# Sums of the way down's blocks: added to the residual on VectorE straight from PSUM

## The chip, the cores and the metric

The kernel runs on one core of a Trainium2 chip. The metric is device time in microseconds (us), the median of three runs. In the profile PE is TensorE's matrix multiplication and PEld its weight loads, DVE is VectorE, ACT ScalarE, POOL GpSimd, SP SyncE (which here only issues transfers). One execution was taken by the hardware profiler; its rows are used below.

## The reference, cut to what matters

One layer of a streaming encoder runs over 1152 tokens (1024 of a new stream and 8 x 16 of running ones): a half step of a gated feed-forward network, a mixer (gated delta rule beside a pooling branch), a second half step, and a final normalization.

```python
x = x + 0.5 * swiglu(rms_norm(x, norm_ffn1), w_ffn1_gate, w_ffn1_up, w_ffn1_down)
x = x + mixer(rms_norm(x, norm_mix), ...)
x = x + 0.5 * swiglu(rms_norm(x, norm_ffn2), w_ffn2_gate, w_ffn2_up, w_ffn2_down)
y = rms_norm(x, norm_final)

def swiglu(x, w_gate, w_up, w_down):
    return (silu(x @ w_gate) * (x @ w_up)) @ w_down
```

The model is 1024 wide and the hidden layer 2816. The change lies in the product with `w_down`, called the way down here, of both half steps, and in the last line, the final normalization.

## The kernel before, in words

Tokens are cut into three chunks: chunk 0 with 512 columns, chunks 1 and 2 with 320 each. Everything is kept transposed, features on the 128 partitions and tokens along the free axis, so the residual is a tile `xk(c, d)` of 128 x 512 or 128 x 320 for each chunk c and feature block d (0 to 7). Every float32 product is made from three products of a reduced type: a weight and an activation are each split into a high part and a remainder (`piece`: an ACT cast at L287 and a DVE subtraction at L288 for weights).

A way down has two halves. `down0` does chunk 0 in the plain way, its sums in the PSUM tag `d`. `down12` does chunks 1 and 2 together by a scheme that makes a 2 x 2 block product from seven products instead of eight (`DOWN` names their seven right sides). It has 12 units: three groups of hidden blocks (`GROUPS`, of 4, 3 and 4) times four feature blocks d. In a unit each of the seven products is 12 matmuls (9 in the middle group) of 128 x 320. Three PSUM tags take them: `a` (`al`, into which four of the products are added one after another, `B11`, `T2`, `T3`, `T4`), `b` (`ga`, product `B21`) and `c` (`be`, products `T1` and then `B22`). After each product the partial sum so far is added to one residual tile: chunk 1 or 2, block d or d + 4, with factor 0.5 or -0.5. Because `al` and `be` go on accumulating, the next product into the same tile starts only after the sum so far has been read.

These seven additions a unit are made in two ways. Five are one DVE instruction that reads PSUM and the residual tile and writes the residual tile (`add`, L652 and L653). Two go another way: after `T1`, ACT copies -0.5 x `be` to a buffer `c3` (L648) and POOL adds it (L649); after `B11`, ACT copies 0.5 x `al` to a buffer `p1` (L677) and POOL adds that (L678). Both buffers lie in region R2 and in Q or A5.

POOL also makes the sums of weight blocks that the scheme needs: three at L282 (the blocks of `T1`, `T3` and `B22`) and one at L286 (for `T2`), four a unit. They need the unit's two weight transfers (`load`), whose buffers come free when the last piece of the unit two before has been split. The product `T1` of the next unit (`fifth`) and `T4` of the one before (`left_low`) are written between the products of the current unit, so each unit's order on PE is T1 of the next unit, T3, B11, B21, T4 of the one before, T2, B22.

`final(c)` does the last line of the reference for chunk c once its squares are summed: `rstd_rest` makes the reciprocal root (two small groups of matmuls with a POOL power between them, L232) and ACT copies it to an SBUF row `r` (L237); then each of the eight tiles is scaled by weight and root, three of them on ACT and POOL (L1568, L1569) and five in one DVE instruction (L1571), and written to `y_out` (L1572). For chunk 0 this is stepped from `beside` inside the second `down12`; for chunks 1 and 2 it is the end of the program.

The order of the instructions on each engine is set by the tile framework's scheduler from the order in which the program names them; each engine then runs its own list strictly in order. `tc.issue_after(ins)` puts the instructions of its block behind `ins` on that instruction's engine.

Of the kernel before, what the change touches and what calls it, by code (L numbers as in the profile page):

```python
# [7 lines left out]
F32 = mybir.dt.float32  # L8
F32R = mybir.dt.float32r
AF = mybir.ActivationFunctionType  # L10
ALU = mybir.AluOpType
# [5 lines left out]
KT = D // P  # L17
# [23 lines left out]
def trunk(ctx: ExitStack, tc: tile.TileContext, xin, s0, convst, poolst, cm_in, vec_in, small_in,  # L41
# [3 lines left out]
    V, A, G, T, SY = nc.vector, nc.scalar, nc.gpsimd, nc.tensor, nc.sync  # L45
# [30 lines left out]
    def pt(tag, shape=None):  # L76
        t = psum.tile([P, 512], F32, tag=tag, name=nm("ps_" + tag))
        return t
# [16 lines left out]
    def region(tag, dt=F32):  # L95
        return main.tile([P, SIZE[tag]], dt, tag=tag, name=nm(tag))
# [17 lines left out]
    def xk(c, k):  # L114
        return X[c][k // 4][:, k % 4, :]
# [149 lines left out]
    N = CHUNKS[1][1]  # L265
    N0 = CHUNKS[0][1]

    class Blocks:
# [5 lines left out]
        def piece(self, *src, more=None):  # L274

            m = src[0].shape[-1]
            t = region(self.ring[self.n % len(self.ring)], F32R)
            self.n += 1
            hi, lo = t[:, :m], t[:, 512:512 + m]
            if len(src) == 2:  # L280
                t = self.gs.get("s", m)
                G.tensor_add(t, *src)  # L282
                src = [t]
            src = src[0]
            if more:
                G.tensor_add(more[0], src, more[1])  # L286
            A.copy(hi, src)  # L287
            V.tensor_sub(lo, src, hi.bitcast(F32))  # L288
            return [x.rearrange("p (k c) -> p k c", c=P) for x in (hi, lo)]

        def product(self, ps, w, hs, start=True, stop=True):
# [316 lines left out]
    def down12(wd, gk, op0, beside, done):  # L608
# [3 lines left out]
        gs, piece, product = bl.gs, bl.piece, bl.product  # L612
        for tag in ("R0", "R1", "O5", "O6"):
            gs.place(region(tag), ("raw", 1024, 1))
        gs.place(region("R2"), ("p1", N, 2), ("c3", N, 1))

        def temps(tag):
            for t in ("s", "sum"):
                gs.mem.pop(t, None)
            gs.mem["c3"] = gs.mem["c3"][:1]  # L620
            gs.place(region(tag), ("s", 512, 2), ("sum", 512, 1), ("c3", N, 1))

        ops = {0: op0}

# [18 lines left out]

        def fifth(g, d, w):

            be, sm, c3 = pt("c")[:, :N], gs.get("sum", w[0].shape[-1]), gs.get("c3", N)
            product(be, piece(w[2], w[3], more=(sm, w[0])), ops[g]["T1"], True, False)
            A.mul(c3, be, -0.5)  # L648
            G.tensor_add(xk(2, d + 4), xk(2, d + 4), c3)  # L649
            return be, sm  # L650

        def add(c, d, ps, by=0.5):  # L652
# [16 lines left out]
        for u, (g, d) in enumerate(units):  # L669
            if not nxt:  # L670
                w = load(g, d, 6)
                nxt = w, fifth(g, d, w)
            (a11, a12, a21, a22), (be, sm) = nxt
            op = ops[g]
            al, ga, p1 = pt("a")[:, :N], pt("b")[:, :N], gs.get("p1", N)
            product(al, piece(a11), op["B11"])
            A.mul(p1, al, 0.5)  # L677
            G.tensor_add(xk(1, d), xk(1, d), p1)  # L678
            product(ga, piece(a12), op["B21"])
            next(beside, None)  # L680
            if last:
# [11 lines left out]
            if u + 1 < len(units):  # L693
# [3 lines left out]
                w = load(g2, d2, 6 if g2 == 0 else 10)  # L697
# [7 lines left out]
            last = g, d, al, a22  # L705
# [749 lines left out]
    for n in names:  # L1455
        if n[1] in "dHXr":
            continue
        b, w, h = n[0], n[1], n[2]
# [79 lines left out]
    squares = {}  # L1538
# [19 lines left out]
    def final(c):  # L1558
        o, n = CHUNKS[c]
        last = c > 0  # L1560
        pool = (2, 5) if last else (1, 4, 7)
        r = nt[c].get("nsq", n)
        pr = yield from rstd_rest(n, squares[c], r)
        yield
        for k in range(KT):
            x, w = xk(c, k), vec[:, 24 + k:25 + k]
            if k in pool:
                A.mul(x, x, w)  # L1568
                G.tensor_tensor(x, x, r, ALU.mult)  # L1569
            else:  # L1570
                V.scalar_tensor_tensor(x, x, w, pr if last else r, ALU.mult, ALU.mult)  # L1571
            (A if last and k in pool else SY).dma_start(y_out[:, o * KT + k * n:o * KT + (k + 1) * n], x)  # L1572
            yield

    downs(wd2, g_keep, x_keep, lambda d: square(0, d), final, square)
# [92 lines left out]
```

## Time and profile before

| | us |
|---|---|
| median of three runs (2211.72 to 2213.26) | 2213.12 |
| the profiled execution | 2211.95 |
| its span, first to last instruction | 2210.2 |
| `down12` of the first half step | about 648 to 790 in the span |
| `down12` of the second half step | about 2040 to 2194 in the span |

The span is what the rows below divide; the profiled execution's own time is 1.75 us longer. A row of the timeline gives the start in the span, the length, the engine, the line of the kernel, the tiles written and read, the count of instructions put together, and in brackets how long the engine sat idle before it and who ended that.

### The profile page before, as it was taken

What the parts mean: (1) busy time and instruction counts of PE and PEld (TensorE: products, weight loads), DVE (VectorE), ACT (ScalarE), POOL (GpSimd) and SP (SyncE); (2) the same over time, 40 slices, a digit from 0 to 9 for tenths busy, and PEclk for the clock granted to TensorE, in tenths of its full rate; (3) what the DMA queues carried; (4) which work ended last, traced back from release to release, by engine and by line L of the source; (5) the groups of instructions that cost most, each with busy time, mean ns of one, the idle gap of its engine ahead of it and who ended that gap; (6) DMA issues with size and microseconds to landing.
All of it is one profiled execution on the core that took longest, in us unless ns stands there. A gap on an engine that the chain in (4) does not pass through costs nothing.

```text
span 2210.2 us, 33211 instructions
## 1 busy us (share of the span) xinstructions
PE 2134.5 (97%) x12341; PEld 1922.0 (87%) x12341; DVE 1519.3 (69%) x2685; ACT 937.0 (42%) x1905; POOL 734.0 (33%) x667
## 2 busy tenths in 40 slices
PE   8999999999999899999999998999999999999997
PEld 7899999998889877787889887889999999988897
DVE  7866666677345867778687867786666668744775
ACT  6433333444223554545444443543333334423343
POOL 1433333440025522322232333143333344101663
PEclk9999999999999999999999999999999999999998
DMA  6332333554555522121222122442333346446561
GB/s 250 114 126 102 130 109 116 182 198 149 189 181 202 190 77 68 49 66 52 77 80 80 44 92 93 135 142 96 124 106 130 109 145 237 141 148 214 183 250 67
DMA packets 102386, 289.72 MB, mean 131 GB/s; under 512 B 16208, under 2 KB 24272, under 8 KB 101968
## 3 DMA queue, kind: packets, MB, share of 16 engines
q1 hardware_dynamic: 101648, 286.94, 38.6%
q8 instruction: 97, 1.59, 0.3%
q10 hardware_dynamic: 576, 0.66, 0.1%
q14 instruction: 65, 0.53, 0.1%
HBM read 214.89 MB, written 72.66 MB: 130 GB/s over the span
## 4 chain that ended last, share of the span: by engine, by line
PE 78%; DVE 10%; issue 3%; POOL 3%; DMA 3%; ACT 2%; DVEq 0%; SPq 0%; POOLq 0%; ACTq 0%
PE ps_a L58 28%; PE ps_b L58 19%; PE ps_d L58 17%; PE ps_c L58 13%; DVE O L288 2%; DMA R<-in_wd 1%; DVE B L982 1%; DVE O L186 1%; DVE A L1122 1%; DVE x L653 1%; PE ps_b L62 1%; DVE A L1324 1%; POOL Q L282 1%; POOL A L282 1%; POOL x L678 1%
## 5 line engine op out<-in xcount | busy, mean ns | idle before, releaser
L58 PE MATMUL ps_a<-B,O 128*128 128x320 f32 x3040 | 510.6, 312 | 16.3 <-DVE x L653 13.2
L58 PEld LDWEIGHTS ps_a<-B,O 128*128 128x128 f32 x3040 | 466.8, 189 | 29.0 <-ACT O L287 15.6
L58 PE MATMUL ps_a<-A,O 128*128 128x320 f32 (+1 forms) x1952 | 426.4, 354 | 3.1 <-DVE A L1122 1.6
L58 PEld LDWEIGHTS ps_a<-A,O 128*128 128x128 f32 x1952 | 330.2, 190 | 37.8 <-issue 3.9
L288 DVE TENSOR_TENSOR O<-Q,O 128x512 fp32r<-128x512 f32 (+1 forms) x238 | 216.5, 913 | 193.6 <-ACT O L287 189.6
L58 PE MATMUL ps_b<-A,O 128*128 128x512 f32 (+1 forms) x1128 | 263.8, 388 | 7.4 <-ACT O L287 7.4
L58 PEld LDWEIGHTS ps_b<-A,O 128*128 128x128 f32 x1128 | 209.0, 189 | 47.1 <-ACT O L287 7.4
L58 PE MATMUL ps_d<-A,O 128*128 128x512 f32 x1056 | 244.1, 391 | 2.3 <-DVE x L602 1.4
L58 PEld LDWEIGHTS ps_d<-A,O 128*128 128x128 f32 x1056 | 196.9, 188 | 48.4 <-issue 3.6
L287 ACT CAST O<-Q 128x512 fp32r<-128x512 f32 (+1 forms) x238 | 143.2, 604 | 187.6 <-POOL Q L282 47.5
L288 DVE TENSOR_TENSOR O<-R,O 128x512 fp32r<-128x512 f32 (+1 forms) x216 | 200.3, 931 | 32.5 <-ACT O L287 31.8
L58 PE MATMUL ps_d<-B,O 128*128 128x320 f32 (+1 forms) x1104 | 205.2, 331 | 5.4 <-DVE x L1003 3.7
L282 POOL TENSOR_TENSOR Q<-R 128x512 f32<-128x512 f32 (+1 forms) x44 | 58.4, 1328 | 433.2 <-DVE O L288 149.0
L287 ACT CAST O<-R 128x512 fp32r<-128x512 f32 (+1 forms) x216 | 130.9, 611 | 134.5 <-PE ps_a L58 54.5
L58 PE MATMUL ps_c<-A,O 128*128 128x512 f32 (+1 forms) x816 | 186.9, 377 | 1.1 <-DVE O L288 1.1
L58 PEld LDWEIGHTS ps_d<-B,O 128*128 128x128 f32 x1104 | 171.2, 189 | 16.0 <-DVE x L1003 6.1
L58 PEld LDWEIGHTS ps_c<-A,O 128*128 128x128 f32 x816 | 145.6, 188 | 25.0 <-DVE O L288 1.9
L185 ACT CAST O<-R 128x1024 fp32r<-128x1024 f32 (+1 forms) x86 | 85.9, 1010 | 183.0 <-PE ps_d L58 136.5
L58 PE MATMUL ps_c<-B,O 128*128 128x320 f32 x912 | 145.8, 310 | 3.0 <-DVE O L288 1.9
L58 PEld LDWEIGHTS ps_c<-B,O 128*128 128x128 f32 x912 | 136.9, 188 | 4.1 <-DVE O L288 2.4
L393 POOL TENSOR_TENSOR A<-A,A 128x512 fp32r<-128x512 f32 x44 | 72.4, 1646 | 161.1 <-ACT A L392 161.0
L186 DVE TENSOR_TENSOR O<-R,O 128x1024 fp32r<-128x1024 f32 (+1 forms) x74 | 87.4, 1188 | 50.3 <-ACT O L185 29.7
(318 smaller groups left out, 3116.4 us busy)
## 6 DMA issues: line engine op xcount, KB each, us to landing
g_keep<-x SPq DMA_DIRECT2D x98, 320.0 KB, 2.5
R<-in_wg SPq DMA_DIRECT2D x48, 512.0 KB, 3.8
R<-in_wd SPq DMA_DIRECT2D x48, 512.0 KB, 3.7
R<-in_wu SPq DMA_DIRECT2D x47, 512.0 KB, 3.7
g_keep<-A SPq DMA_DIRECT2D x44, 512.0 KB, 2.6
A<-g_keep SPq DMA_DIRECT2D x44, 512.0 KB, 5.5
B<-g_keep SPq DMA_DIRECT2D x56, 320.0 KB, 6.6
A<-g_keep SPq DMA_DIRECT2D x42, 320.0 KB, 5.0
```

The lines of the kernel that those rows point to most:

```text
L58: self.put(nc.tensor.matmul(out, lhs, rhs, **k), n / 2400 + .003 if lhs.dtype == F32R else max(n, lhs.shape[-1]) / 600)
L62: self.put(nc.tensor.transpose(out, lhs, rhs), out.shape[-1] / 1200)
L185: A.copy(hi, raw)
L186: (e or V).tensor_sub(lo, raw, hi.bitcast(F32))
L282: G.tensor_add(t, *src)
L287: A.copy(hi, src)
L288: V.tensor_sub(lo, src, hi.bitcast(F32))
L393: G.tensor_sub(go[:, 1], sg, go[:, 0].bitcast(F32))
L653: V.scalar_tensor_tensor(xk(c, d), ps, by, xk(c, d), ALU.mult, ALU.add)
L678: G.tensor_add(xk(1, d), xk(1, d), p1)
L982: V.scalar_tensor_tensor(y[:, :512], raw[:, t:t + 512], cw[:, t:t + 1], y[:, :512], ALU.mult, ALU.add)
L1122: V.tensor_tensor(Uc[:, :, m + 1:], Uc[:, :, m + 1:], tu[:, :n, :w], ALU.add)
```

## The change

Three things change. In `down12` the additions after `T1` and `B11` become `add` like the other five, so all seven are DVE instructions that read PSUM; the two ACT copies and the two POOL additions of a unit go, and with them the buffers `c3` and `p1` (a second buffer `sum` takes the place of one). In `final`, chunk 0 no longer uses ACT and POOL: its eight tiles are all scaled on DVE, each put behind the `piece` subtraction that was named last (`Blocks.mark`), and the step is spread over two more turns of `beside`. At the end of the program three transfers of chunk 1 are issued by ACT instead of SP.

```diff
@@ piece
-            V.tensor_sub(lo, src, hi.bitcast(F32))
+            Blocks.mark = V.tensor_sub(lo, src, hi.bitcast(F32)).ins
@@ down12
-        gs.place(region("R2"), ("p1", N, 2), ("c3", N, 1))
 
         def temps(tag):
             for t in ("s", "sum"):
                 gs.mem.pop(t, None)
-            gs.mem["c3"] = gs.mem["c3"][:1]
-            gs.place(region(tag), ("s", 512, 2), ("sum", 512, 1), ("c3", N, 1))
+            gs.place(region(tag), ("s", 512, 2), ("sum", 512, 2))
@@ down12.fifth
-            be, sm, c3 = pt("c")[:, :N], gs.get("sum", w[0].shape[-1]), gs.get("c3", N)
+            be, sm = pt("c")[:, :N], gs.get("sum", w[0].shape[-1])
             product(be, piece(w[2], w[3], more=(sm, w[0])), ops[g]["T1"], True, False)
-            A.mul(c3, be, -0.5)
-            G.tensor_add(xk(2, d + 4), xk(2, d + 4), c3)
+            add(2, d + 4, be, -0.5)
@@ down12, a unit
-            al, ga, p1 = pt("a")[:, :N], pt("b")[:, :N], gs.get("p1", N)
+            al, ga = pt("a")[:, :N], pt("b")[:, :N]
             product(al, piece(a11), op["B11"])
-            A.mul(p1, al, 0.5)
-            G.tensor_add(xk(1, d), xk(1, d), p1)
+            add(1, d, al)
             product(ga, piece(a12), op["B21"])
@@ final
-        pool = (2, 5) if last else (1, 4, 7)
+        pool = (2, 5) if last else ()
         r = nt[c].get("nsq", n)
-        pr = yield from rstd_rest(n, squares[c], r)
+        root = rstd_rest(n, squares[c], r)
+        next(root)
+        if not last:
+            yield
+            yield
+        yield
+        pr = yield from root
         yield
         for k in range(KT):
             x, w = xk(c, k), vec[:, 24 + k:25 + k]
             if k in pool:
                 A.mul(x, x, w)
                 G.tensor_tensor(x, x, r, ALU.mult)
+            elif last:
+                V.scalar_tensor_tensor(x, x, w, pr, ALU.mult, ALU.mult)
             else:
-                V.scalar_tensor_tensor(x, x, w, pr if last else r, ALU.mult, ALU.mult)
-            (A if last and k in pool else SY).dma_start(y_out[...], x)
+                with tc.issue_after(Blocks.mark):
+                    V.scalar_tensor_tensor(x, x, w, r, ALU.mult, ALU.mult)
+            (A if last and (k in pool or c == 1 and k % 2) else SY).dma_start(y_out[...], x)
             yield
```

The first place is POOL's list at the first units of the first `down12`. Q holds the sums of weight blocks, R and O the raw weights, x the residual; L649 and L678 are the two additions. Before:

```order
L649 TENSOR_TENSOR x_488_5204<-x_488_5204,R_522_5463 128x320
L282 TENSOR_TENSOR Q_5464<-O_521_5462 128x512
L282 TENSOR_TENSOR Q_5464<-R_518_5459,R_519_5460 128x512
L286 TENSOR_TENSOR Q_5464<-Q_5464,O_520_5461 128x512
L678 TENSOR_TENSOR x_485_5201<-x_485_5201,R_522_5463 128x320
L282 TENSOR_TENSOR Q_5464<-Q_5464,O_520_5461 128x512
L649 TENSOR_TENSOR x_488_5204<-x_488_5204,Q_5464 128x320
L282 TENSOR_TENSOR Q_5464<-R_519_5460 128x512
L282 TENSOR_TENSOR Q_5464<-O_520_5461,O_521_5462 128x512
```

Now:

```order
L282 TENSOR_TENSOR Q_5463<-O_521_5462 128x512
L286 TENSOR_TENSOR Q_5463<-Q_5463,O_520_5461 128x512
L282 TENSOR_TENSOR Q_5463<-R_518_5459,R_519_5460 128x512
L282 TENSOR_TENSOR Q_5463<-Q_5463,O_520_5461 128x512
L282 TENSOR_TENSOR Q_5463<-R_519_5460 128x512
L282 TENSOR_TENSOR Q_5463<-O_520_5461,O_521_5462 128x512
L286 TENSOR_TENSOR Q_5463<-Q_5463,R_518_5459 128x512
```

Between the sums of weight blocks nothing is left; two L282 have changed places with an L286.

The second place is DVE's list in the second unit there. L288 is the subtraction of a piece (O is the ring of split weights), L653 an addition from PSUM, which is L650 in the changed kernel. Before, from the piece of the next unit's T1 on:

```order
L288 TENSOR_TENSOR O_550_5706<-Q_5464,O_550_5706 128x512
L653 SCALAR_TENSOR_TENSOR x_485_5201<-ps_b_5614,x_485_5201 128x320
L288 TENSOR_TENSOR O_551_5725<-Q_5464,O_551_5725 128x512
L653 SCALAR_TENSOR_TENSOR x_486_5202<-ps_a_5500,x_486_5202 128x320
L288 TENSOR_TENSOR O_554_5744<-R_518_5459,O_554_5744 128x512
L653 SCALAR_TENSOR_TENSOR x_487_5203<-ps_a_5613,x_487_5203 128x320
L288 TENSOR_TENSOR O_555_5761<-R_518_5459,O_555_5761 128x512
L653 SCALAR_TENSOR_TENSOR x_487_5203<-ps_c_5576,x_487_5203 128x320
L288 TENSOR_TENSOR O_556_5776<-O_521_5462,O_556_5776 128x512
```

Now, from the addition after B11 on:

```order
L650 SCALAR_TENSOR_TENSOR x_485_5201<-ps_a_5609,x_485_5201 128x320
L288 TENSOR_TENSOR O_549_5701<-Q_5463,O_549_5701 128x512
L650 SCALAR_TENSOR_TENSOR x_485_5201<-ps_b_5610,x_485_5201 128x320
L288 TENSOR_TENSOR O_550_5719<-Q_5463,O_550_5719 128x512
L650 SCALAR_TENSOR_TENSOR x_486_5202<-ps_a_5498,x_486_5202 128x320
L288 TENSOR_TENSOR O_553_5738<-R_518_5459,O_553_5738 128x512
L650 SCALAR_TENSOR_TENSOR x_487_5203<-ps_a_5609,x_487_5203 128x320
L288 TENSOR_TENSOR O_554_5754<-R_518_5459,O_554_5754 128x512
L650 SCALAR_TENSOR_TENSOR x_487_5203<-ps_c_5573,x_487_5203 128x320
L288 TENSOR_TENSOR O_555_5769<-O_521_5462,O_555_5769 128x512
```

The addition after B11 (`ps_a_5609`) stands ahead of the piece of the next T1, and the addition after B21 (`ps_b_5610`) behind that piece, as it stood before; the addition after the next T1 (`ps_c`) follows the last piece shown.

The third place is DVE's list in the second `down12`, where chunk 0's tiles are scaled (L1571 before, L1576 now; R is the row of roots). Before:

```order
L653 SCALAR_TENSOR_TENSOR x_1831_17673<-ps_c_17966,x_1831_17673 128x320
L288 TENSOR_TENSOR O_1894_18152<-R_1864_17946,O_1894_18152 128x512
L1571 SCALAR_TENSOR_TENSOR x_1381_12581<-x_1381_12581,vec,R_1841_17742 128x512 x3
L1571 SCALAR_TENSOR_TENSOR x_1382_12582<-x_1382_12582,vec,R_1841_17742 128x512
L288 TENSOR_TENSOR O_1895_18168<-Q_17950,O_1895_18168 128x512
L653 SCALAR_TENSOR_TENSOR x_1832_17674<-ps_a_17986,x_1832_17674 128x320
L288 TENSOR_TENSOR O_1896_18185<-Q_17950,O_1896_18185 128x512
L1571 SCALAR_TENSOR_TENSOR x_1382_12582<-x_1382_12582,vec,R_1841_17742 128x512
L288 TENSOR_TENSOR O_1898_18213<-Q_17950,O_1898_18213 128x512
```

Now:

```order
L288 TENSOR_TENSOR O_1897_18196<-Q_17924,O_1897_18196 128x512
L1576 SCALAR_TENSOR_TENSOR x_1380_12556<-x_1380_12556,vec,R_1840_17717 128x512 x2
L650 SCALAR_TENSOR_TENSOR x_1829_17647<-ps_a_17959,x_1829_17647 128x320
L288 TENSOR_TENSOR O_1900_18217<-R_1862_17920,O_1900_18217 128x512
L650 SCALAR_TENSOR_TENSOR x_1830_17648<-ps_a_18078,x_1830_17648 128x320
L288 TENSOR_TENSOR O_1901_18233<-R_1862_17920,O_1901_18233 128x512
L1576 SCALAR_TENSOR_TENSOR x_1380_12556<-x_1380_12556,vec,R_1840_17717 128x512
L650 SCALAR_TENSOR_TENSOR x_1830_17648<-ps_c_18042,x_1830_17648 128x320
L288 TENSOR_TENSOR O_1902_18250<-O_1865_17923,O_1902_18250 128x512
```

Before, four of the scalings stand together and a fifth three rows later; now there are two and then one, and the other five follow singly, each behind a later piece of the next two units.

## Rows read from the trace of the kernel before

**Rows 1.** Busy us, share and instructions by engine, from the page

```profile
PE 2134.5 (97%) x12341; PEld 1922.0 (87%) x12341; DVE 1519.3 (69%) x2685; ACT 937.0 (42%) x1905; POOL 734.0 (33%) x667
```

**Rows 2.** Stretches: busy us of PE, PEld, DVE, ACT, POOL; clock, DMA, GB/s

```profile
648.00:790.00 142.00, 128.67 (x835) 123.96 (x834) 100.02 (x151) 63.28 (x123) 82.81 (x69) 0.99 0.53 182
...
2040.00:2194.00 154.00, 143.56 (x946) 140.71 (x945) 110.81 (x163) 64.79 (x129) 87.70 (x73) 0.98 0.49 171
```

**Rows 3.** By line, 648:790 us: count | busy, mean ns | idle before

```profile
L58 PE MATMUL ps_a<-B,O 128*128 128x320 f32 x315 | 51.6, 317 | 8.7 <-DVE x L653 7.0 <-ACT O L287 0.8 <-DVE O L288 0.6
...
L58 PE MATMUL ps_c<-B,O 128*128 128x320 f32 x180 | 29.1, 313 | 3.0 <-DVE O L288 1.9 <-ACT O L287 1.1
...
L58 PE MATMUL ps_a<-A,O 128*128 128x320 f32 x144 | 23.4, 310 | 0.8 <-DVE x L653 0.8
...
L58 PE MATMUL ps_c<-A,O 128*128 128x320 f32 x72 | 12.1, 312 | 0.8 <-DVE O L288 0.8
```

**Rows 4.** The same view, 2040 to 2194 us

```profile
L58 PE MATMUL ps_a<-B,O 128*128 128x320 f32 x384 | 63.9, 321 | 7.6 <-DVE x L653 6.2 <-issue 1.2 <-DVE O L288 0.2
```

**Rows 5.** Timeline of one unit: start, us, engine, operation [idle <-releaser]

```profile
667.82 1.11 DVE L288 TENSOR_TENSOR O<-Q,O 128x512 fp32r<-128x512 f32 x1 [4.26 <-ACT O L287]
...
668.35 1.74 POOL L286 TENSOR_TENSOR Q<-Q,R 128x512 f32<-128x512 f32 x1
...
670.05 0.88 POOL L678 TENSOR_TENSOR x<-x,R 128x320 f32<-128x320 f32 x1
...
670.96 0.49 DVE L653 SCALAR_TENSOR_TENSOR x<-ps_b,x 128x320 f32<-128x320 f32 x1 [2.03 <-POOL x L678]
...
674.27 3.75 PE L58 MATMUL ps_a<-B,O 128*128 128x320 f32 x24 [1.76 <-DVE x L653]
```

**Rows 6.** Waits of DVE, 648 to 790 us: total, times, longest us

```profile
DVE x L653 <- POOL x L678: 13.6, 8, 2.0
```

**Rows 7.** Line 653 in the whole span: count, ns min/median/max

```profile
L653 DVE SCALAR_TENSOR_TENSOR x<-ps_a,x x72: 476/478/492, 659.3 to 2194.3; 128x320 f32<-128x320 f32 x72
```

**Rows 8.** Line 288 in the whole span, the same columns

```profile
L288 DVE TENSOR_TENSOR O<-Q,O x238: 541/694/1780, 7.6 to 2128.8; 128x512 fp32r<-128x512 f32 x104, 128x384 fp32r<-128x384 f32 x15
```

**Rows 9.** Timeline of the second way down, 2040 to 2066 us

```profile
2051.08 1.45 POOL L232 TENSOR_TENSOR rt<-rt,vec 128x4 f32<-128x4 f32 x1
...
2052.59 1.16 PE L58 MATMUL ps_d<-ident,rt 128*128 128x128 f32 x8 [2.10 <-POOL rt L232]
...
2054.41 6.59 DVE L1571 SCALAR_TENSOR_TENSOR x<-x,vec,R 128x512 f32<-128x512 f32 x4 [0.74 <-ACT R L237]
...
2063.22 3.07 PE L58 MATMUL ps_a<-B,O 128*128 128x320 f32 x14 [2.43 <-DVE x L653]
```

**Rows 10.** Timeline of its last four units, 2134 to 2180 us

```profile
2148.94 3.76 PE L58 MATMUL ps_a<-B,O 128*128 128x320 f32 x24 [1.16 <-issue]
...
2157.81 3.68 PE L58 MATMUL ps_c<-B,O 128*128 128x320 f32 x24
...
2159.38 0.49 DVE L653 SCALAR_TENSOR_TENSOR x<-ps_b,x 128x320 f32<-128x320 f32 x1 [2.02 <-POOL x L678]
...
2163.64 5.19 PE L58 MATMUL ps_a<-B,O 128*128 128x320 f32 x24 [2.15 <-DVE x L653]
```

**Rows 11.** Timeline of the first way down, 716 to 775 us

```profile
747.33 0.99 POOL L678 TENSOR_TENSOR x<-x,R 128x320 f32<-128x320 f32 x1 [6.68 <-ACT R L677]
...
770.31 0.56 PE L58 MATMUL ps_c<-B,O 128*128 128x320 f32 x2 [1.09 <-ACT O L287]
```

**Rows 12.** Windows of 20 us, columns as in rows 2

```profile
760.00:780.00 20.00, 16.53 (x109) 15.77 (x109) 18.05 (x27) 9.07 (x17) 9.19 (x8) 1.00 0.28 83
...
2060.00:2080.00 20.00, 17.57 (x110) 17.33 (x109) 15.27 (x20) 6.77 (x12) 13.24 (x11) 0.91 0.78 260
```

**Rows 13.** Window over the second group of the second way down

```profile
2096.00:2133.00 37.00, 36.74 (x251) 36.48 (x250) 26.40 (x45) 14.88 (x32) 22.26 (x22) 1.00 0.93 345
```

**Rows 14.** Timeline of the end, 2188 to 2212 us

```profile
2200.43 6.93 SPq L1572 DMA_DIRECT2D out_y<-x  x12
```

More of the change, by code (lines that the diff above doesn't have):

```diff
@@ L1569, in final @@
                 G.tensor_tensor(x, x, r, ALU.mult)
-            else:
-                V.scalar_tensor_tensor(x, x, w, pr if last else r, ALU.mult, ALU.mult)
-            (A if last and k in pool else SY).dma_start(y_out[:, o * KT + k * n:o * KT + (k + 1) * n], x)
+            elif last:
+                V.scalar_tensor_tensor(x, x, w, pr, ALU.mult, ALU.mult)
+            else:
+                with tc.issue_after(Blocks.mark):
+                    V.scalar_tensor_tensor(x, x, w, r, ALU.mult, ALU.mult)
+            (A if last and (k in pool or c == 1 and k % 2) else SY).dma_start(y_out[:, o * KT + k * n:o * KT + (k + 1) * n], x)
             yield
```

## Prediction

> **What bounds the kernel now.** I read the page first, then the windows over the two stretches that the change touches, then what TensorE waited for in them, and last the timeline of single units. The page [rows 1] says that TensorE is busy 97% of the span and VectorE 69%; the reader is to see that there is no engine to relieve over the whole, only waits of TensorE to remove. The windows [rows 2] show where such waits are: TensorE idles 142.0 - 128.7 = 13.3 us in the `down12` of the first half step and 154.0 - 143.6 = 10.4 us in that of the second. VectorE idles 42 and 43 us there. What it lacks is order, not time.
>
> By line [rows 3] the 13.3 us of the first stretch split into 8.7 + 3.0 + 0.8 + 0.8, and 7.0 of them stand before products into `al` that waited for an addition on L653. A unit's timeline shows how that comes about [rows 5]. VectorE gets the piece of the next T1 late (4.26 us idle, the weights had just landed). Next on its list is the addition of the B21 product, which was long there, but its tile `xk(1, d)` is first added to by GpSimd (L678), and GpSimd starts that at 670.05 us, behind its sums of weight blocks (L286 at 668.35). So VectorE idles another 2.03 us until 670.96, everything behind slides, the addition of T2 too, and T3 on TensorE begins at 674.27 after 1.76 us of idling. VectorE met this wait 8 times in the first stretch, 13.6 us in all [rows 6].
>
> The second stretch has the same wait (2.02 us on VectorE at 2159.38, then 2.15 us on TensorE at 2163.64 [rows 10]) and two of its own [rows 9]: 2.10 us until GpSimd made the power of chunk 0's norm, which stood behind its block sums, and 2.43 us after four scalings of chunk 0 had filled VectorE for 6.59 us.
>
> **The change part by part.** The sum is made against the profiled execution, 2211.95 us; the median of the runs is 1.17 us above it.
>
> *The additions that leave GpSimd.* Forty-eight ACT copies and 48 GpSimd additions go. No addition from PSUM waits for GpSimd any more, and in the new list the addition after B11 stands ahead of the piece of T1, on which VectorE idles for the weights. TensorE gets back 7.0 us in the first stretch [rows 3]. In the second, 6.2 us wait for L653; less the 2.43 of the scalings 3.8, of which I take 3.7; to it come the 1.2 put down to issue [rows 4], which stand at the same place of a unit [rows 10]: 4.9.
>
> *Chunk 0's scaling.* The matmuls that need the power are moved behind the unit's other products, some 60 matmuls later, so the power is there in time: 2.1 us. The block of four scalings is cut into single ones: 2.4 us. Together 4.5. They are moved past weight transfers on SP's queue, and SP's output transfers wait for them; but in VectorE's list each scaling comes before the piece that frees the buffer of the weight transfer behind it, so the weights wait for nothing new.
>
> [...]
>
> *GpSimd's shorter list.* GpSimd runs in order, so an addition that waits for its product also holds back sums of weight blocks. At 747.33 us it had idled 6.68 us for one, with block sums behind it; at 770.31 TensorE waited 1.09 us for a piece whose sum came late [rows 11]. Of the first stretch's other waits, 13.3 - 7.0 = 6.3 us, between none and all may go. I take 2.5, the 1.09 and half again as much, since VectorE is busy 18.05 of 20 us there with the mixer's preparation [rows 12].
>
> *What is added.* VectorE gets 24 additions in each stretch, 0.48 us each whatever runs beside them (476 to 492 ns in 72 cases [rows 7]): 11.5 us a stretch, and three more scalings. Their cover is the 42 us of idling [rows 2], 13.6 us of it the very waits that go [rows 6]. In a unit like that at 2157.81 us VectorE then ends the addition of T2 at about the time TensorE comes to T3: idling of 2.02 us goes, 0.48 comes. The cost lies between nothing (or below: a subtraction takes 694 ns at the median and up to 1780 [rows 8], and GpSimd's share of what it collides with is smaller) and 23 us, all 48 on the path. I take 0.3 us in eight units and 0.5 in two of those that hold a scaling: 3.5 us, near the lower end, since the nearest row, the group where VectorE has least room, is 26.4 us of work in 37.0 us [rows 13].
>
> [...]
>
> *The end.* SP issued twelve transfers in 6.93 us [rows 14]; three now go from ACT. The last tile still waits for its scaling, so this saves less than one issue (0.6 us); I count nothing.
>
> *The sum:* 7.0 + 4.9 + 4.5 + 3.0 + 2.5 - 3.5 = 18.4 us, 0.8%. The profiled execution would take 2193.5 us, the median 2194.7.
>
> **The rivals.** *VectorE is full where other work meets the way down.* The mixer's preparation (18.05 of 20 us [rows 12]) and the spread scalings leave no room for the additions: the units before and beside them gain nothing. Then of the first stretch 3.5 us stay (half of 7.0), the 2.5 go to nothing, of the second 4.9 + 2.1 + 1.5, and the 3.5 are paid: 8.5 us, 2204.6. For it speaks that same window; against it, that it holds one unit and a half of twelve.
>
> *Everything goes.* No new wait at all and the rest of GpSimd's delays too: 13.3 of the first stretch, 7.6 + 2.1 of the second [rows 4, 9], 3.0 of clock, 1.5 for a third fall of it: 27.5 us, 2185.6. Against it speak waits there that other engines cause (ACT 0.8 and 1.1, the pieces on L288 [rows 3]).
>
> *Transfers take the time back.* In the middle group the DMA engines are busy 0.93 of the time [rows 13]; a faster first group only reaches the last group's operands sooner and waits for them. Then half of the 7.0 us and the scaling's 4.5 + 1.5 are lost, and 18.4 - 9.5 = 8.9 us remain: 2204.2. Against it: these transfers start when the first group's last products free their buffers, so they move with it.
>
> *VectorE becomes the bound (slower).* A unit's seven additions and seven subtractions stand in one list with a wait for weights in it. In the middle group a unit is 37.0 / 4 = 9.25 us of TensorE and 26.4 / 4 = 6.6 us of VectorE; with two additions 7.6, and with its waits for ACT and weights (4.26 us in rows 5) it is 11.8. From the point where work and wait pass 9.25 us (12.3 in a unit of 12 matmuls a product) each unit pays: 2.6 us in eight units of the middle groups and 0.5 to 1 in the sixteen others make 21 + 12 = 33 against the 21.9 us gained: 11 us slower, 2224. Against it: those waits are met while TensorE still has four products' pieces ready. [...]
>
> **How the numbers follow.** Chances: the forecast 0.60, VectorE full in places 0.17, everything goes 0.10, transfers 0.05, VectorE the bound 0.05, something I don't see 0.03. The likeliest is 2194.7. The range goes from the case in which everything goes to the middle of those that keep a third, 2185.5 to 2206; it leaves out the slower cases and part of the transfers. A measurement tells a change of about 0.2%, 4.4 us. Faster by more: 0.91 (all cases but the last three, and part of the transfers'); within it 0.04; slower 0.05.
>
> **What would show it.** Right: no wait of L650 for GpSimd; TensorE's idling before `al` products that waited for an addition falls from 7.0 and 6.2 us to under 2 in each stretch; no 2 us wait before the matmuls on `rt`; no fall of the clock in the second `down12`; VectorE busier by some 10 us in each stretch with the additions still at 0.48. Wrong: TensorE waiting 1 us or more for L650 in most units, or for the pieces of T1; VectorE busy over 90% through a whole group; scalings of over 1.5 us that hold T3.

## The result, and the profile after

The changed kernel takes 2191.69 us (median of 4 runs, 2188.99 to 2193.70), the kernel before 2212.48 in the same comparison: a ratio of 0.9905, 95% interval [0.9888, 0.9922], 20.8 us less. Forecast were 18.4 us less and 2194.7. The profiled execution takes 2191.8 us, its span is 2190.0.

The page's busy line, to be held against [rows 1]: GpSimd lost 50 us of work, ACT 19, VectorE gained 9.

```profile
PE 2126.5 (97%) x12341; PEld 1917.2 (88%) x12341; DVE 1528.1 (70%) x2736; ACT 918.0 (42%) x1854; POOL 684.1 (31%) x616
```

The windows over the two ways down (columns as in [rows 2]), and one over the start of the mixer, which follows the first. The limits are chosen so that the same matmuls lie in them: 835 in both first stretches, 946 and 944 in the second ones.

```profile
647.00:780.20 133.20, 127.73 (x835) 125.08 (x834) 106.33 (x174) 54.95 (x100) 60.58 (x46) 0.97 0.55 194
...
2028.00:2174.00 146.00, 139.83 (x944) 137.58 (x943) 113.76 (x190) 55.20 (x104) 60.46 (x46) 1.00 0.51 180
...
806.00:823.00 17.00, 15.12 (x79) 12.45 (x80) 10.70 (x20) 10.34 (x20) 3.64 (x6) 1.00 0.21 63
```

The place of the last row in the kernel before:

```profile
816.00:833.00 17.00, 15.11 (x71) 12.35 (x71) 10.55 (x20) 9.53 (x18) 3.64 (x6) 0.90 0.22 62
```

The 20.2 us between the spans come from five places: 1.0 before the first stretch (648.0 against 647.0), 8.8 in it (142.0 against 133.2), 2.2 between the two (1250.0 against 1247.8; at the mixer's start 79 matmuls instead of 71 fit into the same busy time, at a granted clock of 1.00 instead of 0.90), 8.0 in the second (154.0 against 146.0), and 0.2 behind it. Summing the terms by place, with half of the 3.5 us for the added work in each stretch, the forecast had 7.7, none, 10.7 and none from the first stretch on. So the total is right, and the second stretch is not.

Each of these places is read from one execution, and part of it is clock that the change does not set. In the first stretch the mean granted clock was 0.97 instead of 0.99: after a wait of 2.17 us ten matmuls took 3.04 us, at a granted clock of 0.50.

```profile
746.26 3.04 PE L58 MATMUL ps_a<-B,O 128*128 128x320 f32 x10 [2.17 <-DVE O L288]
```

The kernel e1 below runs the same instructions in the same order as the changed kernel up to the second way down. Its profile shows the clock the other way round, 1.00 in the first stretch and 0.90 at the mixer's start:

```profile
646.90:777.40 130.50, 125.33 (x835) 122.43 (x834) 105.24 (x174) 54.90 (x100) 60.57 (x46) 1.00 0.56 198
...
802.00:819.00 17.00, 15.06 (x70) 12.28 (x69) 10.44 (x22) 10.87 (x21) 2.55 (x5) 0.90 0.18 62
```

So the 2.2 us at the mixer's start are no lasting part of the gain, and the first stretch can be 2.7 us shorter with the same instructions. The 1.0 us ahead of it is not an effect either: all kernels of this document run the same instructions there, and the first stretch begins between 646.4 us (e3) and 648.6 us (e10).

What TensorE still waits for, first stretch and then second (total us, times, longest):

```profile
PE ps_a L58 <- DVE x L650: 2.3, 4, 1.1
PE ps_a L58 <- DVE O L288: 2.2, 1, 2.2
...
PE ps_a L58 <- DVE x L650: 5.1, 6, 1.9
PE ps_a L58 <- ACT O L287: 0.6, 1, 0.6
```

The same view of the kernel before, second stretch:

```profile
PE ps_a L58 <- DVE x L653: 6.4, 5, 2.4
```

In the first, waits for additions fell from 7.8 us (7.0 + 0.8 in [rows 3]) to 2.3. In the second they fell only from 6.4 to 5.1. A unit of the first, to be held against [rows 5]:

```profile
663.81 1.29 POOL L282 TENSOR_TENSOR Q<-R 128x512 f32<-128x512 f32 x1 [7.34 <-DMA R<-in_wd]
...
665.79 1.12 DVE L288 TENSOR_TENSOR O<-Q,O 128x512 fp32r<-128x512 f32 x1 [2.93 <-ACT O L287]
...
666.84 0.48 DVE L650 SCALAR_TENSOR_TENSOR x<-ps_b,x 128x320 f32<-128x320 f32 x1
...
670.26 0.48 DVE L650 SCALAR_TENSOR_TENSOR x<-ps_a,x 128x320 f32<-128x320 f32 x1
...
670.97 3.68 PE L58 MATMUL ps_a<-B,O 128*128 128x320 f32 x24
```

VectorE idles 2.93 us for the piece of T1, as before, because GpSimd could begin its sum only when the weights had landed (663.81). But the addition after B21 (666.84) now follows without the wait of 2.03 us, and T3 begins with no idle time instead of 1.76 us. The second stretch has a place where this chain is late again:

```profile
2059.56 1.29 POOL L282 TENSOR_TENSOR Q<-O 128x512 f32<-128x512 f32 x1 [9.15 <-DMA O<-in_wd]
...
2063.90 1.63 POOL L282 TENSOR_TENSOR Q<-Q,O 128x512 f32<-128x512 f32 x1
...
2064.30 1.78 DVE L1576 SCALAR_TENSOR_TENSOR x<-x,vec,R 128x512 f32<-128x512 f32 x1
...
2067.01 0.48 DVE L650 SCALAR_TENSOR_TENSOR x<-ps_a,x 128x320 f32<-128x320 f32 x1
...
2067.63 2.58 PE L58 MATMUL ps_a<-B,O 128*128 128x320 f32 x16 [1.91 <-DVE x L650]
```

A scaling of chunk 0 lies beside a GpSimd sum and takes 1.78 us, as one other of the eight does, where six take 0.74; behind it on VectorE stand the additions after T4 and T2, and T3 waits 1.91 us for them.

### The profile page after: what moved, and what is told of

It is laid out like the page before. It is cut to its first block, busy times and chain, and to the rows that moved or that the text cites. A ratio compares the mean times of both kernels' runs of the same rounds, so it can differ in the third digit from the quotient of the medians.

```text
span 2190.0 us, 33160 instructions
## 1 busy us (share of the span) xinstructions
PE 2126.5 (97%) x12341; PEld 1917.2 (88%) x12341; DVE 1528.1 (70%) x2736; ACT 918.0 (42%) x1854; POOL 684.1 (31%) x616
## 4 chain that ended last, share of the span: by engine, by line
PE 79%; DVE 11%; DMA 3%; issue 2%; POOL 2%; ACT 2%; DVEq 0%; SPq 0%; POOLq 0%; ACTq 0%
PE ps_a L58 28%; PE ps_b L58 19%; PE ps_d L58 17%; PE ps_c L58 13%; DVE O L288 2%; DVE x L650 1%; DMA R<-in_wd 1%; DVE B L978 1%; POOL Q L282 1%; DVE A L1118 1%; DMA O<-in_wd 1%; DVE O L186 1%; PE ps_b L62 1%; DVE A L1320 1%; DMA B<-g_keep 1%
## 5 line engine op out<-in xcount | busy, mean ns | idle before, releaser
L288 DVE TENSOR_TENSOR O<-Q,O 128x512 fp32r<-128x512 f32 (+1 forms) x238 | 209.7, 882 | 192.1 <-ACT O L287 191.2
L288 DVE TENSOR_TENSOR O<-R,O 128x512 fp32r<-128x512 f32 (+1 forms) x216 | 198.5, 923 | 33.0 <-ACT O L287 32.1
L282 POOL TENSOR_TENSOR Q<-R 128x512 f32<-128x512 f32 (+1 forms) x44 | 57.7, 1311 | 448.1 <-DMA R<-in_wd 284.2
```

The costliest lines, as they stand in the source:

```text
L288: Blocks.mark = V.tensor_sub(lo, src, hi.bitcast(F32)).ins
```

## The experiments

Each kernel was timed against the kernel before on the same chip. "Gain" is the distance of the two medians there; what a run loses against the changed kernel is told as a difference of gains.

| kernel | us | ratio, 95% interval | gain |
|---|---|---|---|
| changed kernel | 2191.69 | 0.9905 [0.9888, 0.9922] | 20.8 |
| e1_add | 2193.39 | 0.9916 [0.9902, 0.9929] | 18.5 |
| e2_scaling | 2214.30 | 1.0011 [1.0002, 1.0020] | -2.4 |
| e3_b11_only | 2200.23 | 0.9948 [0.9934, 0.9963] | 11.6 |
| e4_t1_only | 2206.17 | 0.9979 [0.9968, 0.9989] | 5.7 |
| e5_mark | 2189.91 | 0.9905 [0.9892, 0.9919] | 21.2 |
| e6_t1_piece_later | 2196.08 | 0.9934 [0.9921, 0.9946] | 15.0 |
| e7_more_sum_buffers | 2200.98 | 0.9958 [0.9944, 0.9972] | 10.1 |
| e8_additions_twice | 2195.83 | 0.9934 [0.9921, 0.9946] | 15.3 |
| e9_scaling_after_sums | 2213.42 | 1.0012 [1.0003, 1.0021] | -2.2 |
| e10_sums_from_copies | 2195.53 | 0.9939 [0.9926, 0.9952] | 15.7 |
| e11_mark_five_raw | 2184.52 | 0.9883 [0.9870, 0.9896] | 26.8 |
| e12_mark_t2sum_vectore | 2189.73 | 0.9904 [0.9889, 0.9920] | 21.5 |

**The two halves of the change (e1_add, e2_scaling).** e1 is the changed kernel with `final` as before; e2 is the kernel before with the new `final` and its mark.

> Only the forty-eight additions move to VectorE; chunk 0's scaling stays as it was. Theory (the additions after B11 stopped waiting behind GpSimd's sums of weight blocks): 7.0 + 4.9 + 2.5 of waits and 1.5 of clock, less 2.5 to 3.0 for the added work, about 13 us faster, near 2199.5; the waits of 2.1 us for the power and about 2.4 us behind the burst of four scalings stay in the trace, and TensorE's waits for additions in the first stretch fall from 7.8 us to the 2.3 us of the changed kernel. Rival (most of the 20.8 us measured came from the scaling, and VectorE has no room for the additions): at most 6 us faster, 2206 or more. Rival (the two parts only pay together, since GpSimd's and ACT's scalings hold the list): under 9 us.

> Only the scaling of chunk 0 and the transfers at the end change; the additions after T1 and B11 stay with ACT and GpSimd. Theory: 2.1 (power) + 2.4 (burst) + 1.5 (clock) = 6.0 us faster, about 2206.5, and the first stretch keeps its 13.3 us of idling. Since in the changed kernel one scaling took 1.78 us beside a GpSimd sum and TensorE waited 1.9 us behind it, up to 2 of the 6 may be missing: 2206.5 to 2208.5. Rival (the idle time is not worth its length; what is late next takes it): under 2 us, above 2210.

The additions alone bring 18.5 us, more than the 13 expected; the scaling alone loses 2.4. The theory's sizes fell in both runs, and of the rivals only the one for e2 (the idle time is not worth its length) stands. What the additions took of the other part's share is seen in e1's timeline, where `final` is as before:

```profile
2037.50 1.16 PE L58 MATMUL ps_d<-ident,rt 128*128 128x128 f32 x8 [1.09 <-POOL rt L232]
...
2039.32 3.60 DVE L1567 SCALAR_TENSOR_TENSOR x<-x,vec,R 128x512 f32<-128x512 f32 x2
...
2043.24 1.39 DVE L1567 SCALAR_TENSOR_TENSOR x<-x,vec,R 128x512 f32<-128x512 f32 x1
...
2046.88 1.99 PE L58 MATMUL ps_a<-B,O 128*128 128x320 f32 x12 [1.19 <-DVE x L650]
...
2049.17 2.00 PE L58 MATMUL ps_a<-B,O 128*128 128x320 f32 x12 [0.30 <-DVE x L650]
```

The wait for the power is 1.09 us instead of 2.10 [rows 9], and those behind the scalings are 1.19 + 0.30 instead of 2.43: 1.9 of the 4.5 us go without any new scaling. GpSimd's list before the power is shorter by an addition, and on VectorE the block of four scalings [rows 9] is broken up: two stand together, the next (2043.24) follows an addition. So the expectation that both waits would stay was wrong as well. And e2's timeline shows where its own gain went:

```profile
2059.30 1.12 DVE L288 TENSOR_TENSOR O<-Q,O 128x512 fp32r<-128x512 f32 x1 [3.92 <-ACT O L287]
...
2062.45 0.49 DVE L653 SCALAR_TENSOR_TENSOR x<-ps_b,x 128x320 f32<-128x320 f32 x1 [2.03 <-POOL x L678]
...
2067.73 3.76 PE L58 MATMUL ps_a<-B,O 128*128 128x320 f32 x24 [2.51 <-DVE x L653]
2068.11 0.74 DVE L1580 SCALAR_TENSOR_TENSOR x<-x,vec,R 128x512 f32<-128x512 f32 x1
...
2069.88 0.34 SPq L641 DMA_DIRECT2D O<-in_wd  x1
...
2073.52 1.30 POOL L282 TENSOR_TENSOR Q<-O 128x512 f32<-128x512 f32 x1 [6.88 <-DMA O<-in_wd]
...
2082.90 5.28 PE L58 MATMUL ps_a<-B,O 128*128 128x320 f32 x24 [2.61 <-DVE x L653]
```

The waits of 2.10 and 2.43 us are gone, and two new ones of 2.51 and 2.61 stand in the next two units, the second with slow matmuls behind it (24 in 5.28 us). What is late there are weights. The second transfer of a unit (L641) waits for the piece that frees its buffer, and the scaling at 2068.11 stands ahead of that piece on VectorE; GpSimd then idles 6.88 us until the weights land. These transfers are issued at 2053.81, 2069.88 and 2085.04 us, 16.1 and 15.2 us apart. In the kernel before they are issued at 2053.69, 2072.53 and 2084.67: 18.8 us pass in the unit with the two waits and 12.1 in the next, GpSimd begins its sum at 2076.54 without waiting for weights, and TensorE is busy without a pause soon after:

```profile
2072.53 0.34 SPq L641 DMA_DIRECT2D O<-in_wd  x1
...
2076.54 1.30 POOL L282 TENSOR_TENSOR Q<-O 128x512 f32<-128x512 f32 x1
...
2084.67 0.34 SPq L641 DMA_DIRECT2D R<-in_wd  x1
```

```profile
2080.00:2100.00 20.00, 20.00 (x138) 20.00 (x137) 13.81 (x22) 7.72 (x15) 9.96 (x10) 1.00 0.31 98
```

**Which of the two additions (e3_b11_only, e4_t1_only).** In e3 the lines of `fifth` are as before, in e4 those after `B11`:

```diff
 e3, in fifth
-            add(2, d + 4, be, -0.5)
+            A.mul(c3, be, -0.5)
+            G.tensor_add(xk(2, d + 4), xk(2, d + 4), c3)
 e4, in a unit
-            add(1, d, al)
+            A.mul(p1, al, 0.5)
+            G.tensor_add(xk(1, d), xk(1, d), p1)
```

> The changed kernel, but the addition after T1 goes through an ACT copy and GpSimd again; the addition after B11 stays on VectorE. Theory (what VectorE waited for was the addition after B11, 13.6 us in eight waits in the first stretch): this keeps most of the gain, within 4 us of the changed kernel, 2191.7 to 2196. Rival (GpSimd's list is what counts: it waited 19 us in the first stretch for the copy after T1 and 6.7 us for the one after B11): it loses most of the additions' gain, 2199 or more.

> The changed kernel, but the addition after B11 goes through an ACT copy and GpSimd again; the addition after T1 stays on VectorE. Theory: the waits of VectorE for GpSimd come back, eight of about 1.7 us in each first stretch, and 8 to 13 us of the gain go: 2200 to 2205. Rival (GpSimd's list counts, and the copy after T1 was what held it): within 4 us of the changed kernel, 2191.7 to 2196.

Giving T1's addition back to GpSimd costs 9.2 us (20.8 - 11.6), giving B11's back 15.1. Both matter, so neither theory holds as it stood: e3 lost more than the 4 us that its theory allowed, e4 more than the 8 to 13. Together they lose more than the two additions bring, so the losses overlap. In e4 VectorE waits for GpSimd as before (first stretch):

```profile
DVE x L651 <- POOL x L677: 12.0, 6, 2.0
```

In e3 it has no such wait. Of the 8.7 us between e3's profiled span and the changed kernel's, 5.0 lie between the two ways down (1252.8 us instead of 1247.8), which e3's edit does not touch. There the clock at the mixer's start is 0.70, and 55 matmuls lie in the busy time that holds 79 in the changed kernel:

```profile
805.00:822.00 17.00, 15.05 (x55) 12.06 (x54) 8.50 (x18) 9.58 (x18) 2.26 (x4) 0.70 0.10 31
```

**The place of a scaling (e5_mark, e9_scaling_after_sums).** In e5 `Blocks.mark` is the last addition, not the last subtraction, in the changed kernel; in e9 the same in e2's kernel.

```diff
-            Blocks.mark = V.tensor_sub(lo, src, hi.bitcast(F32)).ins
+            V.tensor_sub(lo, src, hi.bitcast(F32))
 add
-            V.scalar_tensor_tensor(xk(c, d), ps, by, xk(c, d), ALU.mult, ALU.add)
+            Blocks.mark = V.scalar_tensor_tensor(xk(c, d), ps, by, xk(c, d), ALU.mult, ALU.add).ins
```

> The changed kernel, but each scaling of chunk 0 is put behind the last addition instead of behind the last subtraction of a piece, so that it no longer stands ahead of the two additions that T3 waits for. Theory (a scaling of 1.78 us ahead of T2's addition is what held T3 for 1.9 us at 2067.63 us of the changed kernel's span, and the same place costs smaller waits in other units): 2 to 3 us faster than the changed kernel, 2188.5 to 2190, and no wait of TensorE over 1 us for an addition between 2045 and 2080 us. Rival (the scalings need VectorE's time wherever they stand): no difference, 2191 to 2192.5.

> The kernel before with the new scaling of chunk 0 (as in the run that changed the scaling alone), but each scaling stands behind the last addition on VectorE instead of behind the last subtraction. Theory (the scaling alone lost 2.4 us because a scaling of 1.4 us stood ahead of the two additions that T3 waits for, 2.5 us of waiting at 2067.7 and 2.6 us at 2082.9 us of that run's span): the forecast of 6.0 us for this part comes out at least by half, 2206 to 2209. Rival (eight scalings on VectorE cost their time wherever they stand while GpSimd makes two additions a unit): no better than the scaling alone, 2212 or more.

In e5 the mechanism showed as expected: between 2045 and 2080 us TensorE waits for nothing at all, and its waits for additions in the second stretch fall from 5.1 us to

```profile
PE ps_a L58 <- DVE x L650: 2.3, 3, 1.5
```

Its time was inside the expected 2188.5 to 2190, though the gain of 21.2 us can't be told from 20.8. In e9 the theory fell: it is as slow as e2, though its scalings stand behind the additions. (What it calls a scaling of 1.4 us in e2 were two of 0.7.) The timeline says why:

```profile
2069.03 0.33 SPq L641 DMA_DIRECT2D O<-in_wd  x1
...
2073.94 1.29 POOL L282 TENSOR_TENSOR Q<-O 128x512 f32<-128x512 f32 x1 [6.09 <-DMA O<-in_wd]
...
2079.72 1.09 DVE L288 TENSOR_TENSOR O<-Q,O 128x512 fp32r<-128x512 f32 x1 [2.69 <-ACT O L287]
...
2082.36 5.19 PE L58 MATMUL ps_a<-B,O 128*128 128x320 f32 x24 [3.15 <-DVE x L653]
```

The weights are issued at 2069.03 us and land at 2073.94; GpSimd idled 6.09 us for them, its sums come late, VectorE idles for the pieces made from these, and T3 waits 3.15 us for an addition behind them. The new theory from here, which e11 tests: what each unit waits for in the end are its weights, and a stall taken out ahead of them only moves the wait to the next unit.

**VectorE's order, GpSimd's buffers, the price (e6, e7, e8).** e6 puts the subtraction of T1's piece behind T2's addition, e7 gives GpSimd's sums four buffers instead of two, e8 makes each added addition twice.

```diff
 e6, in fifth
+            with tc.issue_after(late) if late else nullcontext():
+                hs = piece(w[2], w[3], more=(sm, w[0]))
-            product(be, piece(w[2], w[3], more=(sm, w[0])), ops[g]["T1"], True, False)
+            product(be, hs, ops[g]["T1"], True, False)
 e7, in temps
+            gs.place(region("R2"), ("s", 512, 2))
 e8, after the two additions
+            V.scalar_tensor_tensor(gs.get("scr", N), be, -0.5, xk(2, d + 4), ALU.mult, ALU.add)
+            V.scalar_tensor_tensor(gs.get("scr", N), al, 0.5, xk(1, d), ALU.mult, ALU.add)
```

> The changed kernel, but the subtraction of the next unit's T1 piece stands behind the addition of T2 in VectorE's list, so that VectorE no longer idles for weights with additions behind it. Theory (what is left of TensorE's waits for additions, 2.3 us in the first and 5.1 us in the second stretch, comes from that order): 3 to 7 us faster than the changed kernel, 2185 to 2189. Rival (T1's product, which TensorE takes up right after, gets late in its place, and each unit waits for its piece): 5 us or more slower, 2197 and above. Rival (nothing, since the wait for weights sets the unit's start in any case): within 2 us of 2191.7.

> The changed kernel with four buffers instead of two for GpSimd's sums of weight blocks (in the region that the two old buffers left). Theory (GpSimd idled 30.3 and 15.2 us in the first stretch until VectorE had read a sum, and TensorE's wait of 2.2 us at 746 us with the fall of the clock behind it came from sums that were late): 2 to 5 us faster than the changed kernel, 2187 to 2190. Rival (GpSimd runs ahead only as far as the weights have landed, and earlier sums collide with VectorE's subtractions elsewhere): within 2 us, or slower.

> The changed kernel with each of the forty-eight added additions made twice, the second time into a buffer that nothing reads: 24 more instructions of 0.48 us on VectorE in each stretch. Theory (their cover is VectorE's idling): they cost about what the prediction counted for the first forty-eight, 3.5 us, and since the room is less now up to twice that: 2194 to 2199. Rival (VectorE is at its bound in a unit): 0.3 to 0.5 us for each, 14 to 23 us, 2206 to 2215. Rival (fully hidden): within 2 us.

e6 loses 5.8 us of the gain, so its theory fell and its first rival stands, if with 2196.1 us just under the 2197 that it had. The waits for additions nearly go, and others come, for the pieces of T1 (tag `c`), in the first stretch and in the second:

```profile
PE ps_c L58 <- DVE O L288: 3.5, 3, 2.1
...
PE ps_c L58 <- DVE O L288: 5.8, 7, 1.9
PE ps_d L58 <- POOL rt L232: 1.7, 2, 1.2
PE ps_a L58 <- DVE x L652: 0.4, 1, 0.4
```

So this order of VectorE's list moves the wait from one product to another. e7 loses 10.7, and its theory fell too. In the first stretch GpSimd's sums wait 3.3 us for VectorE instead of 45.5, but 69.7 us for weights instead of 30.4, and in one unit they then run without a pause beside the subtractions:

```profile
760.87 1.24 DVE L288 TENSOR_TENSOR O<-A,O 128x512 fp32r<-128x512 f32 x1 [1.84 <-ACT O L287]
...
761.64 1.63 POOL L282 TENSOR_TENSOR R<-A,R 128x512 f32<-128x512 f32 x1
...
762.44 1.39 DVE L209 TENSOR_TENSOR A<-A 128x512 f32<-128x512 f32 x1
763.24 1.73 POOL L282 TENSOR_TENSOR A<-R,R 128x512 f32<-128x512 f32 x1
763.75 1.77 DVE L288 TENSOR_TENSOR O<-R,O 128x512 fp32r<-128x512 f32 x1
...
767.66 1.67 PE L58 MATMUL ps_a<-B,O 128*128 128x320 f32 x5 [3.52 <-DVE x L651]
```

L209 and L288 take 1.39 and 1.77 us there (0.68 alone), and T3 waits 3.52. That place does not make up e7's loss: of the 12.1 us between its profiled span and the changed kernel's, 2.4 lie in the first stretch, 4.0 in the second and 5.5 between the two (1253.3 us instead of 1247.8), where the clock at the mixer's start is 0.70, as in e3. e8 took 2195.8 us, inside the 2194 to 2199 that were expected, and loses 5.5 us for 48 instructions; the rival of 14 us and more fell.

**Reading PSUM, the weights, a sum moved (e10, e11, e12).** In e10 VectorE adds ACT's copies from SBUF; e11 is e5 with a fifth raw buffer; e12 is e5 with the sum for T2 on VectorE.

```diff
 e10, the two additions
+            A.mul(c3, be, -0.5)
+            V.tensor_add(xk(2, d + 4), xk(2, d + 4), c3)
+            A.mul(p1, al, 0.5)
+            V.tensor_add(xk(1, d), xk(1, d), p1)
 e11, in down12
-        for tag in ("R0", "R1", "O5", "O6"):
+        for tag in ("R0", "R1", "O5", "O6", "R2"):
 e12, in piece, called with eng=V in fifth
-                G.tensor_add(more[0], src, more[1])
+                (eng or G).tensor_add(more[0], src, more[1])
```

> The changed kernel, but the two additions of a unit read ACT's copy in SBUF instead of PSUM: the copies are back, GpSimd has none of the additions. Theory (what paid was that additions left GpSimd's list): within 3 us of the changed kernel, 2189 to 2195. Rival (that VectorE reads PSUM is what pays, since an instruction with two SBUF inputs is held up by a GpSimd sum beside it as the subtractions are, 0.68 us against 1.38): a third to a half of the 48 additions take up to 0.9 us longer, 5 to 15 us slower, 2197 to 2207.

> The run with the scaling behind the last addition (2189.9 us) with a fifth buffer for raw weights, so that one of a unit's two transfers can be issued earlier. Theory (each unit's start is set by weights that have just landed: VectorE idles 16.2 us in the first stretch for pieces made from them): 1 to 4 us faster, 2186 to 2189. Rival (sums and subtractions that start earlier collide with the additions that T3 waits for, as with more buffers for the sums): slower, 2193 or more.

> The run with the scaling behind the last addition (2189.9 us), and the sum of weight blocks for T2 (one of GpSimd's four a unit) is made on VectorE, 24 instructions in all. Theory (a GpSimd sum of 1.3 to 1.75 us holds up a VectorE subtraction by about 0.7 us, so that VectorE loses as much time to it as making the sum itself would take): within 2 us, 2188 to 2192, with subtractions of over 1.2 us rarer by a quarter. Rival (VectorE's room is what counts, 48 additions more cost 4.1 us): 24 sums of about 0.68 us cost 3 to 6 us, 2193 to 2196.

e10 keeps 15.7 of the 20.8 us, between the two theories: most of the gain is that additions left GpSimd's list, and some 5 us hang on reading PSUM, be it the wait for ACT's copy (VectorE idled 4.8 us for it in the first stretch) or the company of GpSimd; the two were not separated, and the profile is of its slowest run, 2200.83 us. Its additions after B11 (count, ns min/median/max) take up to 1.58 us; the longest of the changed kernel's 168 took 0.492.

```profile
L678 DVE TENSOR_TENSOR x<-x,R x24: 477/493/1584, 655.4 to 2172.4; 128x320 f32<-128x320 f32 x24
```

e11 is the fastest of all, 26.8 us under the kernel before; its slowest run (2185.05) lies under the fastest of the changed kernel (2188.99). VectorE's idling for pieces fell from 18.3 us in e5 to 5.3 in the first stretch, and in the second TensorE is busy 142.85 of 143.00 us:

```profile
DVE O L288 <- ACT O L287: 5.3, 16, 1.8
```

```profile
2024.00:2167.00 143.00, 142.85 (x970) 141.75 (x969) 122.53 (x191) 57.53 (x105) 60.79 (x46) 1.00 0.52 180
```

VectorE does 122.53 us of work in these 143, and TensorE waits 0.2 us for it: the idle time was the weights', not a lack of room. e12 is as fast as e5, as its theory had it; of the 164 subtractions in the two ways down 18 instead of 28 took over 1.2 us, and that was worth nothing that can be measured, so the collisions that went lie off the path.

## Why the prediction was right, and where it was not

**The sum** came out (20.8 against 18.4), but two terms were off in opposite directions: the main mechanism, additions that waited behind GpSimd's sums, was right, and that the total came so near was luck.

*Additions that leave GpSimd (7.0 + 4.9), GpSimd's shorter list (2.5), less the added work (3.5).* Right in kind, too small. With one of the two returns of the clock they made about 13 us, and e1 measured 18.5. The first stretch is right by place: 8.8 us against 7.7 (11.5 in e1), no wait of VectorE for GpSimd left, waits for additions down by 5.5 us, TensorE's other waits down from 5.5 (13.3 - 7.8) to 3.2 us (133.20 - 127.73 - 2.3), which is near the list's 2.5. The working given for that term does not make 2.5, though: 1.09 and half again as much are 1.6. What was mis-sized is, first, the addition after T1, to which I gave only the list's 2.5: e3 puts it at 9.2 us, more than half of it clock by the profile. Second, the additions also shorten the waits that I had given to the scaling, by 1.9 us (e1). Third, the clock did not fall at all in e1's first stretch (1.00 instead of 0.99), which was not forecast and, since the changed kernel's own profile shows 0.97 there, is not a sure part of the gain.

*Chunk 0's scaling (4.5).* This step failed. The waits of 2.10 and 2.43 us did go, and e2 and e9 lost them again, and 2.4 and 2.2 us besides, in the next units, wherever the scalings stood. The reason that the prediction gave, that each scaling comes before the piece that frees a weight buffer, so that "the weights wait for nothing new", is what went wrong: that piece comes later by the scaling ahead of it, and the transfer with it. The larger error was to price the two waits at their length. While TensorE was held up by them, the weights of the units behind caught up (18.8 us between two transfers), and it then ran 20.00 us of 20; without them the transfers of e2 came 16.1 and 15.2 us apart, where TensorE could take a unit in 12.1. Two or three scalings of 0.7 us are a small part of that; the rest is the round of transfer, sum and piece, in e2 with GpSimd's additions still in it. This is akin to the rival "transfers take the time back" (0.05), though that spoke of the last group's operands and not of the weights. In the changed kernel the part brings 2.3 us (20.8 - 18.5), which can't be told from nothing. The sign that I named for it stood in the trace: one scaling of 1.78 us that held T3 for 1.91.

*The clock (3.0).* The term is 1.5 us for each of two waits, and the 1.5 in the rivals' sums is the same figure: 24 matmuls took 5.19 us behind a wait of 2.15, 24 others 3.68 [rows 10]. The granted clock was 0.50 from 2164 to 2166 us there and 1.00 over the others. A second fall stood behind the wait of 2.43 us (0.91 over 20 us [rows 12]). That such a wait sets off the fall, and that 1.5 us come back for each, was an estimate: no run shows the term by itself, and in the changed kernel the clock is 1.00 from 2063 to 2080 us, with a wait of 1.91 us in it. What the runs show in its place is the second stretch as a whole, and there it was right: 946 matmuls took 143.56 us of TensorE before, 944 take 139.83, at 1.00 instead of 0.98. e1, with the scaling as before, has 1.00 there as well. For the first stretch nothing was forecast, and the clock fell from 0.99 to 0.97.

*What is added (3.5).* The first 48 can't be priced by themselves; 48 more cost 5.5 us (e8), which fits the choice near the lower end, and "VectorE becomes the bound" was far off. (The units as counted, eight of 0.3 and two of 0.5 us, make 3.4.) VectorE was not some 10 us busier in each stretch, as the signs had it, but 6.3 and 3.0 [rows 2]: the subtractions of the pieces took 131.6 us in the two stretches instead of 140.0. In the two stretches of the changed kernel the subtractions and scalings of 128 x 512, which read two tiles in SBUF, took up to 1.78 us beside a GpSimd sum and 0.67 to 0.74 alone, and its additions, which read PSUM, never over 0.492. What the long ones cost is not shown: in e12 18 instead of 28 took over 1.2 us, and its gain (21.5 us) can't be told from e5's (21.2).

*The signs.* Of those named, four came: no wait of L650 for GpSimd, none before the matmuls on `rt`, a clock of 1.00 in the second way down, additions of 0.48 us. Two did not: VectorE's busy time, and waits for additions under 2 us in each stretch (2.3 and 5.1; 2.3 in the second with e5's order).

*The end.* 16.0 us behind the second stretch instead of 16.2: nothing, as said.

**What stays open:** why the clock at the mixer's start was 1.00 in the changed kernel, 0.90 before and in e1, and 0.70 in e3 and e7; how much of the losses of e3 and e7 a second profile would show as clock; and whether the new scaling pays by itself once there are five raw buffers, which wasn't tried.

## What to carry to other kernels

A wait that you take away is worth its length only where the next late input has slack: follow each wait past the engine that is named (here an addition) to the one that idled before it, until you reach a transfer or TensorE itself. Where that is a transfer, a buffer that lets it start earlier can be worth more than another order of the instructions behind it: here it brought 5.6 us (26.8 - 21.2, e11 against e5), while the orders tried brought nothing that can be measured (e5) or cost time (e6). Price the halves of a change apart: a right total can hide two wrong terms.

## What the runs showed of the hardware

The granted clock made differences here as large as a wait: the 835 matmuls of the first stretch took 127.73 us at 0.97 in the changed kernel and 125.33 at 1.00 in e1. It did so also where the change does not reach: 17 us at the mixer's start held 79, 71 or 55 matmuls in 15.1 us of busy time, at 1.00 (changed kernel), 0.90 (before) and 0.70 (e3, e7). It was not settled by the instructions alone: the changed kernel and e1 run the same ones in the same order up to there and had 1.00 and 0.90. The four runs of the changed kernel lie in the order of their mean granted clock, from 2188.99 us at 0.996 to 2193.70 at 0.993. Small losses (e3, e7) are therefore not read as waits alone.

Sums that GpSimd could begin earlier did not make the kernel faster: e7 lost 10.7 us of the gain. In its trace sums fell beside VectorE's two-input instructions (L288 took 1.77 us instead of 0.68), but nearly half of the loss lies between the two ways down, so these collisions are not shown to be its cause.
